# The last expert's outputs kept on the chip: moving gates, loads and return products in a two-block transformer kernel

## The chip, the cores and the metric

The kernel runs on one core of a Trainium2 chip. The metric is the device time of one execution in microseconds (us), taken as the median of three runs. TensorE (PE) multiplies matrices, VectorE (DVE) and ScalarE (ACT) work on elements, GpSimd (POOL) issues indirect transfers, and SyncE (SP) issues the loads and stores in the order in which they stand in its queue.

## The reference: what is computed

The program is two blocks with float32 inputs, model width 1024 and 256 tokens. The second block also carries 256 context tokens. It runs an even mixer (neighbourhood attention and an mLSTM), a first mixture of experts (MoE) over all 512 rows, an odd mixer (attention with grouped queries), and a second MoE over the 256 latent rows. Each MoE has 16 experts, of which a row uses two:

```python
w = jnp.take_along_axis(scores, e_idx, axis=-1)
w = w / w.sum(axis=-1, keepdims=True)
comb = (jax.nn.one_hot(e_idx, N_EXPERTS) * w[..., None]).sum(axis=1)
y = jnp.zeros_like(h)
for e in range(N_EXPERTS):
    y = y + comb[:, e:e + 1] * ((jax.nn.silu(h @ w1[e]) * (h @ w3[e])) @ w2[e])
...
x_lat = x_lat + g2 * y_lat          # in the first MoE: x_ctx = x_ctx + cg2 * y_ctx too
```

So each expert's output row is multiplied with a routing weight and with a gate vector (`g2` for latent, `cg2` for context rows) before it is added to the row's residual `x`.

## The kernel before

The first MoE (`moe_gather`, line 1765) gives each expert 96 slots. For each expert it gathers the rows' inputs from `hbuf` in device memory (`X`, an indirect DMA that GpSimd issues), transposes them (`xtp`, `XT`), multiplies them with four 1 MB slices of `w1` and `w3` into `ph` (slots 0 to 63) and `pq` (slots 64 to 95), applies the SwiGLU gate (`ga`, `gq`), transposes again (`gT`), and multiplies with two 1 MB slices of `w2` into `py` and `pyq`. ScalarE copies these into `ysb` (128x512) and `ysq` (128x256), and SP stores both into `ybuf` in device memory (lines 1834 and 1841). The weights lie in a ring of 18 slots of 1 MB (`SLOTS0`), filled by `wload` (line 343) on the SP queue, in which the two stores of every expert stand too.

The outputs come back per row: `fetch` (line 1852) gathers each row's first expert (`G`, four tiles of 128 rows) after expert 14's store, and its second expert (`qT`, `kT`, `v`) after expert 15's store. `combine` weights a tile with `wn` and the gate (`g2`, line 1860; one tile on ScalarE and GpSimd, lines 1863 and 1864) and adds it to `x` or `xc` (line 1865). Then the odd mixer starts: sum of squares per row on ScalarE (line 390), a power on GpSimd (lines 392 and 394), a diagonal matrix `diag` of the row scales (line 314), transposes of the scaled rows (`htp`), and the projection products `pt`. Its weights are split into a high part `wh` (ScalarE, line 368) and a low part `wl` (VectorE, line 369) in `stream`; the first of them are loaded in six pieces.

The second MoE (`moe_onehot`, line 1880) works without gathers: one-hot matrices bring rows to slots (`px`) and back. `second` makes an expert's weighted output `Y` as a high and a low part, and `back` (line 1975) adds a pair of experts to `x` by products `yc` of K=64 rows: expert rows 0 to 63 of the array hold one half of the columns, rows 64 to 127 the other. `back` is called after the odd expert's `Y`, in the middle of the next expert.

The order on each engine is set by a scheduler that goes by priority and readiness; `issue_after` ties an instruction behind another.

## Time and profile before

| what | us |
|---|---|
| median of three runs | 1564.82 (1559.56 to 1565.23) |
| the profiled execution | 1561.84 |
| its span, first to last instruction | 1560.1 |
| PE busy | 1419.2 (91% of the span) |
| DVE busy | 718.0 (46%) |
| ACT busy | 438.7 (28%) |
| POOL busy | 154.2 (10%) |

The even mixer lies at about 490 to 760 us, the first MoE at 765 to 1117, the odd mixer with its start at 1117 to 1290, and the second MoE from 1290 to the end. A row of a timeline gives start, duration, engine and line, the operation with its output and inputs, the shapes and the count, and in brackets the idle time before it and what ended that. Matrix products are pipelined, so the distance between two starts says more than a duration.

### The profile page before, as it was taken

The numbers are of one execution on the slowest core, as the hardware profiler recorded it, in microseconds if no ns is written. First come the engines' busy times: TensorE is split into PE (matmuls) and PEld (weight loads), VectorE is DVE, ScalarE is ACT, GpSimd is POOL, SyncE is SP. The second block draws the span as 40 slices with busy tenths as digits, with TensorE's granted clock in tenths as the row PEclk, the third lists the DMA queues.
The fourth block names the chain that finished last, engine by engine and source line by source line (L and its number), as shares of the span: only waits on it lengthen the run. The fifth ranks groups of instructions, "written<-read, shape, count | busy, mean of one in ns | idle before, by whom it ended". The sixth has DMA issues, their size and how long they took to land.

```text
span 1560.1 us, 24539 instructions
## 1 busy us (share of the span) xinstructions
PE 1419.2 (91%) x10110; PEld 927.2 (59%) x10110; DVE 718.0 (46%) x1609; ACT 438.7 (28%) x881; POOL 154.2 (10%) x217
## 2 busy tenths in 40 slices
PE   8999999999999998989489999986549998999997
PEld 7576787768888885959433333332238785434342
DVE  4756544866654657365512111011166755333333
ACT  4334332344543324243211111012124432111110
POOL 2100120002101312000110000000142000000000
PEclk9999999999999999989789999998859998999999
DMA  8677675676723112124599878877543528999890
GB/s 298 233 295 284 229 249 174 235 286 231 233 67 95 53 33 79 55 86 158 218 342 338 323 282 325 325 297 298 197 159 109 223 89 317 419 421 418 332 376 30
DMA packets 65703, 359.23 MB, mean 230 GB/s; under 512 B 13027, under 2 KB 16349, under 8 KB 26793
## 3 DMA queue, kind: packets, MB, share of 16 engines
q1 hardware_dynamic: 57680, 335.04, 57.4%
q0 software_dynamic: 5824, 19.68, 3.9%
q10 hardware_dynamic: 2073, 2.79, 0.5%
q8 instruction: 84, 1.38, 0.3%
q14 instruction: 42, 0.34, 0.1%
HBM read 344.77 MB, written 12.71 MB: 229 GB/s over the span
## 4 chain that ended last, share of the span: by engine, by line
PE 37%; DMA 9%; DVE 2%; ACT 1%; issue 1%; SPq 0%; POOL 0%; ACTq 0%; POOLq 0%; DVEq 0%
PE ph L270 14%; PE py L270 6%; DMA w<-in_w_dram 5%; PE pt L270 4%; PE pq L270 3%; DMA ybuf<-ysq 2%; PE yc L270 2%; PE gtp L293 1%; PE px L270 1%; PE pyq L270 1%; PE poG L270 1%; PE lgG L270 1%; PE xtp L293 1%; DMA w<-in_odd_w_dram 1%; PE htp L270 0%
## 5 line engine op out<-in xcount | busy, mean ns | idle before, releaser
L270 PE MATMUL ph<-w,XT 128*64 128x512 f32 x1024 | 256.6, 616 | 28.0 <-DMA w<-in_w_dram 13.9
L369 DVE TENSOR_TENSOR wl<-w,wh 128x2048 fp32r<-128x2048 f32 (+2 forms) x74 | 152.1, 2058 | 104.6 <-ACT wh L368 103.9
L270 PE MATMUL pt<-wh,hT 128*128 128x256 f32 x640 | 187.0, 293 | 0.6 <-ACT hT L368 0.5
L270 PE MATMUL pt<-wl,hT 128*128 128x256 f32 x640 | 185.2, 290 | 1.7 <-DVE wl L369 1.7
L270 PE MATMUL pt<-wh,hTl 128*128 128x256 f32 x640 | 183.2, 290 | 0.7 <-POOL hTl L369 0.2
L368 ACT CAST wh<-w 128x2048 fp32r<-128x2048 f32 (+2 forms) x74 | 127.1, 1719 | 138.5 <-PE pt L270 48.5
L270 PEld LDWEIGHTS ph<-w,XT 128*64 128x64 f32 x1024 | 70.1, 139 | 152.5 <-issue 128.0
L270 PE MATMUL pf<-hT,wh 128*128 128x256 f32 (+1 forms) x480 | 141.5, 299 | 0.3
L270 PE MATMUL pf<-hT,wl 128*128 128x256 f32 (+1 forms) x480 | 140.5, 294 | 1.0 <-DVE wl L369 0.9
L270 PE MATMUL pf<-hTl,wh 128*128 128x256 f32 (+1 forms) x480 | 141.3, 295 | 0.0
L1753 DVE SCALAR_TENSOR_TENSOR ga<-ga,ph 64x512 f32<-64x512 f32 x32 | 21.7, 679 | 235.6 <-ACT ga L1752 235.6
L270 PEld LDWEIGHTS pt<-wl,hT 128*128 128x128 f32 x640 | 123.9, 194 | 9.1 <-issue 5.9
L270 PEld LDWEIGHTS pt<-wh,hT 128*128 128x128 f32 x640 | 123.9, 194 | 8.9 <-issue 4.8
L270 PEld LDWEIGHTS pt<-wh,hTl 128*128 128x128 f32 x640 | 122.9, 193 | 4.4 <-issue 2.6
L270 PE MATMUL py<-w,gT 128*64 128x512 f32 x512 | 121.6, 596 | 1.3 <-DVE gT L1826 0.8
L270 PEld LDWEIGHTS pf<-hT,wh 128*128 128x128 f32 x480 | 91.5, 192 | 11.1 <-issue 4.7
L270 PEld LDWEIGHTS pf<-hT,wl 128*128 128x128 f32 x480 | 92.0, 192 | 7.6 <-issue 2.9
L270 PEld LDWEIGHTS pf<-hTl,wh 128*128 128x128 f32 x480 | 92.1, 192 | 5.5 <-issue 4.2
L270 PEld LDWEIGHTS py<-w,gT 128*64 128x64 f32 x512 | 37.0, 137 | 68.0 <-issue 65.5
L270 PE MATMUL ada<-w,cT 128*32 128x512 f32 x384 | 73.2, 612 | 0.1
L270 PE MATMUL pq<-w,XT 128*32 128x256 f32 x1024 | 72.1, 384 | 0.0
L270 PE MATMUL pt<-wh,yT 128*128 128x256 f32 x256 | 62.6, 289 | 0.0
(525 smaller groups left out, 2136.9 us busy)
## 6 DMA issues: line engine op xcount, KB each, us to landing
w<-in_w_dram SPq DMA_DIRECT2D x192, 1024.0 KB, 12.9
w<-in_ada_w_dram SPq DMA_DIRECT2D x48, 1024.0 KB, 7.2
w<-in_w_in_dram SPq DMA_DIRECT2D x30, 1024.0 KB, 7.3
w<-in_even_w_dram SPq DMA_DIRECT2D x12, 1024.0 KB, 4.8
w<-in_w_out_dram SPq DMA_DIRECT2D x8, 1024.0 KB
w<-in_even_out_dram SPq DMA_DIRECT2D x4, 1024.0 KB, 4.8
ybuf<-ysb SPq DMA_DIRECT2D x16, 256.0 KB
w<-in_odd_w_dram SPq DMA_DIRECT2D x4, 1024.0 KB, 5.0
```

What stands on the lines that cost most here:

```text
L270: self.last = self.nc.tensor.matmul(out, lhsT, rhs, start=start, stop=stop)
L293: self.nc.tensor.transpose(out, in_, self.cst["ident"][:k, :k])
L368: self.nc.scalar.copy(hi, src)
L369: (self.nc.vector if eng == "v" else self.nc.gpsimd).tensor_tensor(out=lo, in0=src, in1=hi.bitcast(F32), op=ALU.subtract)
L1753: nc.vector.scalar_tensor_tensor(g, g, 1.0, ph[0:n], op0=ALU.add, op1=ALU.mult)
```

## The change

In the first MoE, VectorE now applies routing weight and gate to an expert's slots when it reads `py` and `pyq` (`gated`: two fused products and a sum, with the weights of latent and of context rows, `wt`, computed in `route`). The gates per slot (`gs`) are loaded once by twelve DMAs on GpSimd's queue into the ring's slot `hold[2]`, so the ring has 17 slots. The gathers of `X` are issued three experts ahead in the code. Expert 15 is stored no more: its outputs stay in `ysb` and `ysq`, one-hot matrices `oh`, transposed to `ohT`, bring them to the rows by products `yl`, and `x` adds those from PSUM. All eight gathers `G` are issued after expert 14's store; a row that has no slot among the stored ones gets a row of zeros. The odd mixer's first loads and their splits are tied behind the last expert's weights and gates. In the second MoE, `back` issues the products of the two halves of the array in turn, and its call moves behind the first products of the following expert. In the even mixer, `side_by_side` gets a 1x1 product that waits for the bank of a pair (`banks`).

```diff
-SLOTS0 = lambda ...: ... + wx(rz + rx[5:] + hold[1:3])
+SLOTS0 = lambda ...: ... + wx(rz + rx[5:] + hold[1:2])
+YROW = 5 * P
...
-    def side_by_side(self, *streams, after=None):
-        for group in zip(*streams):
-            for m in reversed(group):
-                with self.tc.issue_after(after) if after else ExitStack():
-                    after = self.mm(*m).ins
+    def side_by_side(self, *streams, banks=(), after=None):
+        one = self.cst["ones"][:, :1]
+        for m in [(b[:1, :1], one, one, True, True) for b in banks] + [m for group in zip(*streams) for m in reversed(group)]:
+            with self.tc.issue_after(after) if after else ExitStack():
+                after = self.mm(*m).ins
...
# stream: the first three units of the odd weights
+                with ExitStack() as c:
+                    for ins in after if n < 3 else ():
+                        c.enter_context(self.tc.issue_after(ins))
...
# even mixer, the pair cmb[0], cmb[1]
-                                    for d in range(2)))
+                                    for d in range(2)), banks=cmb[:1])
...
# moe_gather
+            Xs = [fetch_in(e) for e in range(XBUFS)]
+            gs = self.hold[2].tile([P, 2 * D], F32, tag="wx", name="gs")
...
+                        nc.gpsimd.dma_start(g[m * j:m * j + m, w], self.mod[l][w:w + 1, ...].to_broadcast([m, n]))
...
+            def gated(y, py, i, e):
+                g, wt, n = gates[i], self.wt[i], y.shape[-1]
+                yt = T([P, 512], "yt", 1)[:, :n]
+                nc.vector.scalar_tensor_tensor(y, py, wt[:, 0, e:e + 1], g[:, 0], op0=ALU.mult, op1=ALU.mult)
+                nc.vector.scalar_tensor_tensor(yt, py, wt[:, 1, e:e + 1], g[:, 1], op0=ALU.mult, op1=ALU.mult)
+                return nc.vector.tensor_add(y, y, yt).ins
...
-                self.copy(ysb, py, "s")
+                gated(ysb, py, 0, e)
+                if e < NE - 1:
+                    nc.sync.dma_start(self.ybuf[r0:r0 + 64]..., ysb)
...
                 if e == NE - 2:
-                    self.combine_first(l)
-            with self.tc.issue_after(last.ins):
-                for t in range(NT - 1):
-                    self.combine(0, t, self.first[t // 2][:, t % 2], nc.vector)
+                    G = self.fetch_all(NT, rx)
+            self.behind = [self.loaded, shown, gated_]
+            for t in range(NT):
+                with self.tc.issue_after(gated_):
+                    for c in range(2):
+                        nc.vector.tensor_add(xs[t], xs[t], G[c][t // 2][:, t % 2])
+                pos = [self.psum(("lg", "pj")[t % 2], name="yl") for _ in range(2)]
+                for part, (src, n) in enumerate(((ysb, 512), (ysq, 256), (ysq, 256))):
+                    for j in range(2):
+                        q = slice(64 * j, 64 * j + 64)
+                        self.mm(pos[j][:, ...], ohT[q, t, part * P:(part + 1) * P], src[q], part == 0, part == 2)
+                for j in range(2):
+                    nc.vector.tensor_add(o, o, pos[j])       # o: x's columns j
...
# odd_mixer
-            for t in range(4):
-                got = self.fetch(1, t, G[t])
-            with self.tc.issue_after(got.ins):
-                self.combine(0, 3, self.first[1][:, 1], nc.gpsimd)
...
-                self.combine(1, t, g, nc.vector)
...
# moe_onehot
-            def back(pr, owT, Y):
+            def back(pr, owT, Y, after=None):
                 for t in range(NT):
+                    pos = [self.psum(POT[j], name="yc") for j in range(2)]
+                    r = [slice(64 * j, 64 * j + 64) for j in range(2)]
+                    after = self.side_by_side(*([(pos[j], owT[r[j], t, i], Y[i][n][r[j]], i + n == 0, i + n == 2)
+                                                 for i in range(2) for n in range(2)] for j in range(2)), after=after)
...
                     last = hidden(e, tiles[pr][0], w13, 0, ph)
+                    if e % 2 and pr:
+                        back(pr - 1, tiles[pr - 1][1], Ys[-2:], last.ins)
...
-                        if e % 2 == 0:
-                            back(pr - 1, tiles[pr - 1][1], Ys[-2:])
```

The first place where instructions stand otherwise is the SP queue at the end of the first MoE, between the store of expert 11's `ysq` and that of expert 14's. Before:

```order
L1841 DMA ybuf<-ysq 4x32x256
L343 DMA w<-in_w_dram 128x2048 x2
L357 DMA w<-in_odd_w_dram 128x512 x4
L357 DMA w<-in_odd_w_dram 128x1024 x2
L1834 DMA ybuf<-ysb 2x64x512
L343 DMA w<-in_w_dram 128x2048 x2
L1841 DMA ybuf<-ysq 4x32x256
L357 DMA w<-in_odd_w_dram 128x2048
L1834 DMA ybuf<-ysb 2x64x512
L1841 DMA ybuf<-ysq 4x32x256
L357 DMA w<-in_odd_w_dram 128x2048 x2
```

The same stretch of the SP queue now:

```order
L1888 DMA ybuf<-ysq 4x32x256
L345 DMA w<-in_w_dram 128x2048 x4
L1880 DMA ybuf<-ysb 2x64x512
L1888 DMA ybuf<-ysq 4x32x256
L1880 DMA ybuf<-ysb 2x64x512
L1888 DMA ybuf<-ysq 4x32x256
L363 DMA w<-in_odd_w_dram 128x512 x4
L1880 DMA ybuf<-ysb 2x64x512
L363 DMA w<-in_odd_w_dram 128x1024
L1888 DMA ybuf<-ysq 4x32x256
L363 DMA w<-in_odd_w_dram 128x1024
L363 DMA w<-in_odd_w_dram 128x2048
```

The last two slices of expert 15's `w2` stood behind the six odd pieces and a store; now the last four slices of expert 15 stand together, and odd pieces and the stores of experts 12 to 14 follow them.

The second place is VectorE after the last expert. Before, each gathered tile was weighted and then added:

```order
L1826 COPY gT<-gtp 128x4x64
L1860 SCALAR_TENSOR_TENSOR G_10691<-G_10691,wn,g_10688 128x1024
L1865 TENSOR_TENSOR x<-x,G_10691 128x1024
L1860 SCALAR_TENSOR_TENSOR G_10691<-G_10691,wn,g_10688 128x1024
L1860 SCALAR_TENSOR_TENSOR G_10698<-G_10698,wn,g_10688 128x1024
L1865 TENSOR_TENSOR x<-x,G_10691 128x1024
L1865 TENSOR_TENSOR xc<-xc,G_10698 128x1024
L1860 SCALAR_TENSOR_TENSOR qT<-qT,wn,g_10688 128x1024
```

Now, from the last expert's gating of `pyq` on:

```order
L1838 TENSOR_TENSOR ysq<-ysq,yt 128x256
L1897 TENSOR_TENSOR x<-x,G 128x1024 x2
L1897 TENSOR_TENSOR xc<-xc,G 128x1024
L375 TENSOR_TENSOR wl<-w,wh 128x512 x4
L375 TENSOR_TENSOR wl<-w,wh 128x1024 x2
L1897 TENSOR_TENSOR x<-x,G 128x1024 x2
L1897 TENSOR_TENSOR xc<-xc,G 128x1024 x2
L1906 TENSOR_TENSOR x<-x,yl 128x512 x4
L1897 TENSOR_TENSOR xc<-xc,G 128x1024
L1906 TENSOR_TENSOR xc<-xc,yl 128x512 x4
L314 TENSOR_SCALAR hfull<-htp,modA,modc 128x128 x4
```

The weighting is gone, the six odd splits stand between the third and the fourth addition of a gathered tile, and sixteen additions end before the first feature.

The third place is TensorE within a pair of experts of the second MoE; the number behind `Y` tells the expert and the high or low part apart, and lines left out hold other products. Before:

```order
L270 MATMUL yc<-Y_12799,owT 128x512
L270 MATMUL yc<-Y_12800,owT 128x512
...
L270 MATMUL ph<-w,XT 64x512 x5
L270 MATMUL yc<-Y_12934,owT 128x512 x2
L270 MATMUL yc<-Y_12935,owT 128x512 x2
L270 MATMUL yc<-Y_12934,owT 128x512
L270 MATMUL yc<-Y_12935,owT 128x512
L270 MATMUL ph<-w,XT 64x512 x3
```

Now:

```order
L271 MATMUL ph<-w,XT 64x512 x10
L271 MATMUL yc<-Y_13261,owT 128x512 x2
L271 MATMUL yc<-Y_13262,owT 128x512 x2
L271 MATMUL ph<-w,XT 64x512
...
L271 MATMUL yc<-Y_13396,owT 128x512 x2
L271 MATMUL yc<-Y_13397,owT 128x512 x2
L271 MATMUL yc<-Y_13261,owT 128x512
L271 MATMUL py<-w,gT 64x512 x8
...
L271 MATMUL yc<-Y_13261,owT 128x512
L271 MATMUL yc<-Y_13262,owT 128x512 x2
```

An `x2` is now a product on the array's upper rows beside one on its lower rows with the same `Y`. Sixteen products, which stood in groups of 4, 2, 6 and 4, stand in groups of 4, 5 and 7; one product at the end of the second group has its partner at the head of the third.

## Rows read from the trace of the kernel before

**Rows 1.** stretches: busy us (count) per engine, granted clock, DMA share, GB/s

```profile
490.00:565.00 75.00, 75.00 (x527) 63.52 (x526) 44.93 (x114) 26.77 (x48) 20.22 (x40) 1.00 0.14 44
860.00:900.00 40.00, 40.00 (x348) 16.05 (x350) 7.33 (x14) 5.60 (x13) 1.90 (x2) 1.00 0.88 328
1081.70:1092.81 11.11, 0.00 (x0) 0.00 (x0) 4.96 (x6) 5.94 (x10) 0.00 (x0) 0.68 0.66 240
1116.80:1160.02 43.22, 5.83 (x20) 4.65 (x21) 22.27 (x21) 8.62 (x18) 17.39 (x19) 0.53 0.56 198
1330.00:1460.00 130.00, 127.97 (x743) 53.49 (x741) 49.63 (x102) 19.81 (x38) 0.00 (x0) 1.00 1.00 416
1460.00:1524.00 64.00, 61.82 (x358) 25.23 (x356) 20.96 (x36) 9.22 (x18) 0.00 (x0) 1.00 0.84 329
```

**Rows 2.** chain that ended last, 950 to 1072: start, us, what

```profile
1040.63 1.94 PE ph L270 x8
...
1045.88 15.82 DMA w<-in_w_dram
...
1061.84 3.59 PE ph L270 x8
```

**Rows 3.** the same chain from 1070 to 1162

```profile
1080.46 10.11 DMA w<-in_odd_w_dram
...
1117.20 18.94 DMA ybuf<-ysq
...
1141.72 3.80 DVE qT L1860
```

**Rows 4.** timeline of VectorE: start, us, what, count, idle before and releaser

```profile
1086.80 2.60 DVE L369 TENSOR_TENSOR wl<-w,wh 128x512 fp32r<-128x512 f32 x4 [20.11 <-ACT wh L368]
1090.40 2.50 DVE L369 TENSOR_TENSOR wl<-w,wh 128x1024 fp32r<-128x1024 f32 x2 [0.99 <-ACT wh L368]
1092.81 0.67 DVE L1753 SCALAR_TENSOR_TENSOR ga<-ga,ph 64x512 f32<-64x512 f32 x1
...
1137.21 1.22 DVE L1865 TENSOR_TENSOR xc<-xc,G 128x1024 f32<-128x1024 f32 x1
```

**Rows 5.** timeline of GpSimd, the gathers of the first and second expert

```profile
1124.19 1.02 POOL L1852 DMA_INDIRECT G<-ybuf,sidx  x1 [113.49 <-DMA g<-mod]
...
1137.00 1.16 POOL L1852 DMA_INDIRECT qT<-ybuf,sidx  x1 [7.90 <-DMA ybuf<-ysq]
1138.47 0.99 POOL L1852 DMA_INDIRECT qT<-ybuf,sidx  x1 [0.30 <-issue]
```

**Rows 6.** the gathers of the experts' inputs X, last line of that tile's view

```profile
DMA to landing us min/median/max: 4.7/9.2/14.9
```

**Rows 7.** timeline of ScalarE ahead of the odd mixer

```profile
1146.85 1.06 ACT L390 ACTIVATE qT<-x 128x1024 f32<-128x1024 f32 x1 [9.69 <-DMA v<-ybuf,sidx]
...
1156.00 0.40 ACT L314 ACTIVATE diag<-cpack,nrmr 128x128 f32<-128x128 f32 x1 [1.96 <-POOL nrmr L394]
```

**Rows 8.** timeline of TensorE, the odd mixer's first projection product

```profile
1160.02 0.56 PE L270 MATMUL pt<-wh,hT 128*128 128x256 f32 x1
```

**Rows 9.** timeline of TensorE, one pair of experts in the second MoE

```profile
1350.22 1.20 PE L270 MATMUL yc<-Y,owT 64*128 64x512 f32 x6
1351.35 1.50 PE L270 MATMUL ph<-w,XT 128*64 128x512 f32 x5
...
1356.76 1.19 PE L270 MATMUL yc<-Y,owT 64*128 64x512 f32 x4
1357.88 1.51 PE L270 MATMUL px<-oh,xn 128*128 128x128 bf16 x24
...
1366.71 0.71 PE L270 MATMUL yc<-Y,owT 64*128 64x512 f32 x2
1367.35 1.08 PE L270 MATMUL ph<-w,XT 128*64 128x512 f32 x4
```

**Rows 10.** timeline of TensorE, one cmb product of the even mixer

```profile
511.86 1.12 PE L270 MATMUL cmb<-cm,cpack 32*128 32x512 f32 x2
```

More of the change, by code (lines that the diff above doesn't have):

```diff
@@ L39 @@
 BEHIND = (9,)
-FOLLOW = (15, 16, 17)
+FOLLOW = (15, 16)
 H2S = 1
@@ L344, in wload, with stream @@
         return t
-    def stream(self, units):
+    def stream(self, units, after=()):
         nc = self.nc
@@ L1800, in moe_gather @@
                                              bounds_check=NT * P - 1, oob_is_err=False)
+                return X
+            Xs = [fetch_in(e) for e in range(XBUFS)]
+            gs = self.hold[2].tile([P, 2 * D], F32, tag="wx", name="gs")
+            gates = []
+            for m, o in ((64, 0), (32, D)):
+                n = m * 8
+                g = gs[:, o:o + 2 * n].rearrange("p (w f) -> p w f", w=2)
+                for w in range(2):
+                    for j in range(P // m):
+                        nc.gpsimd.dma_start(g[m * j:m * j + m, w], self.mod[l][w:w + 1, 5 * D + n * j:5 * D + n * (j + 1)].to_broadcast([m, n]))
+                gates.append(g)
+            rel = self.last_slots(sidx, C, NT)
+            def gated(y, py, i, e):
[4 more added lines that the diff above has]
+                return nc.vector.tensor_add(y, y, yt).ins
+            for e, (w13, w2) in enumerate(weights):
+                X = Xs.pop(0)
                 XT = T([P, KD, C], "XT", 2)
@@ new lines, in last_onehot @@
+    def last_onehot(self, rel, NT, p0, p1):
+        nc, iota = self.nc, self.cst["iota128"]
+        oh, ohT = (p.tile([P, NT, 3 * P], F32, tag="wx", name=n) for p, n in ((p0, "oh"), (p1, "ohT")))
+        nc.gpsimd.memset(oh, 0.0)
+        for c0, n, i in ((0, 64, 0), (P, 32, 0), (2 * P, 32, 32)):
+            for j in range(2):
+                o = c0 + 64 * j + i
+                s0 = 0 if n == 64 else 64
+                nc.vector.tensor_tensor(oh[:, :, o:o + n], iota[:, None, s0:s0 + n].to_broadcast([P, NT, n]),
+                                        rel.unsqueeze(2).to_broadcast([P, NT, n]), op=ALU.is_equal)
+        for t in range(NT):
+            tp = self.psum("tp", name="ohtp")
+            for i in range(3):
+                self.tr(tp[:, i * P:(i + 1) * P], oh[:, t, i * P:(i + 1) * P])
+            self.copy(ohT[:, t], tp[:, :3 * P], "s")
+        return ohT
@@ new lines, in fetch_all @@
+    def fetch_all(self, NT, rx):
+        G = [[rx[2 * c + w].tile([P, 2, D], F32, tag="wx", name="G") for w in range(2)] for c in range(2)]
+        n = YROW + (NE - 1) * CAP
+        for t in range(NT):
+            for c in range(2):
+                self.nc.gpsimd.indirect_dma_start(out=G[c][t // 2][:, t % 2], out_offset=None, in_=self.ybuf[:n],
+                                                  in_offset=bass.IndirectOffsetOnAxis(ap=self.sidx[:, c, t:t + 1], axis=0),
+                                                  bounds_check=n - 1, oob_is_err=False)
+        return G
@@ L2004, in moe_onehot @@
                     last = hidden(e, tiles[pr][0], w13, 0, ph)
+                    if e % 2 and pr:
+                        back(pr - 1, tiles[pr - 1][1], Ys[-2:], last.ins)
                     if e:
```

116 lines of the change are left out of this document (63 added, 53 removed).

## The prediction, made before the changed kernel was run

> **What bounds the kernel now.** I read the stretches first, then the chain of waits, then the timelines where the chain leaves TensorE.
>
> In the first MoE TensorE is full at first (40.00 of 40 us at 860 to 900 [rows 1]). Later it waits for weights: the chain goes through loads that take 15.8 us from issue to landing, and the experts follow each other at the pace of the transfers, from 1040.63 to 1061.84, 21.2 us [rows 2]. Where only weights move, the rate is 416 GB/s [rows 1], so 1 MB (1.049 million bytes) takes 2.52 us and an expert's six loads 15.1. The other 6.1 us of a period are what the two stores of its outputs cost the queue. They move 0.38 MB, but hold back what is behind them far longer than their bytes.
>
> At the end of this MoE come two stretches with TensorE nearly empty. From 1081.70 to 1092.81 it does nothing [rows 1]: the six odd pieces, the last of which lands at 1080.46 + 10.11 = 1090.57 [rows 3], occupy ScalarE and VectorE (2.60 and 2.50 us of splits [rows 4]) ahead of the last experts' gates. From 1116.80 to 1160.02 it works 5.83 us of 43.22, at a clock of 0.53 [rows 1]: expert 15's store takes 18.94 us [rows 3], gathers, weighting and adding follow, and the first projection starts at 1160.02 [rows 8].
>
> In the second MoE TensorE is full (127.97 of 130 us, then 61.82 of 64), while the transfers run at 1.00 until 1460 and at 0.84 after it [rows 1]. None of its waits there is for a load.
>
> **The change part by part.**
>
> *Gating in slots.* ScalarE's copies go. VectorE gets three operations for each half: 3 x 0.67 us for 512 columns by the nearest form [rows 4], less for 256. VectorE is busy 7.33 us of 40 at 860 to 900 [rows 1], so this hides beside TensorE. The stores are ready about 1.5 us later; with 15.8 us between issue and landing of the loads [rows 2] the transfers do not run dry. I take zero. The twelve loads of `gs` are about 0.79 MB, 1.9 us at 416 GB/s; small rows make it 2.5 by my estimate (0 if they fill gaps, 5 at twice my value). These add to a transfer stream that sets the end.
>
> *One slot fewer, gathers three ahead.* Three buffers of `X` were used before too, so the gathers gain nothing. A slot fewer costs at most one load of 2.52 us where the ring is full at the start; later the loads are late, not the slots. I take 0 (0 to +2.5).
>
> *Odd loads behind the last weights.* The last `w2` slice of expert 15 now lands at 1090.57 - 5.0 (2 MB of odd pieces) + 5.0 (the two `w2` slices that stood behind them) + 2.5 (gates) = 1093.1. TensorE is no longer blocked by splits at 1081.70 to 1092.81; what is late next is these slices, and I put the end of expert 15 near 1107 instead of 1116.80 (the 24.0 us from 1092.81 on, less some 10 for first products and expert 14's outputs that are done by then). This alone does not set the odd mixer's start.
>
> *The return.* The store of 18.94 us, its gathers, and the weighting (3.80 us for the first tile, which ran beside GpSimd's product [rows 3]) leave the chain. What is late next is expert 14's store. Behind 1093.1 stand three pairs of stores (3 x 6.1 = 18.3) and 1.5 MB of odd pieces (3.8): it lands at 1115.2. Before, the first gather started at 1124.19 after the same store [rows 5]. Now eight gathers start at 1116.0, 1.3 us apart (0.99 and an idle 0.30 [rows 5]), and land 9.2 us after issue, as those of `X` do among loads [rows 6]: the fifth at 1130.4, the eighth at 1134.3.
>
> VectorE's order makes the rest: the addition of the fifth gather ends at 1131.7, then the six splits 5.1 us [rows 4] to 1136.8, four additions of 1.2 [rows 4] to 1141.6, four `yl` additions of 512 columns at 0.67 to 1144.3, one of 1.2 to 1145.5, four of 0.67 to 1148.2. ScalarE takes the sums of squares of all four tiles before the first `diag`, so both `diag` of `x` come after 1.3 us more (1.06 [rows 7], and a little to read the sum out), at 1149.5. From the second `diag` to the first `pt` it was 1156.00 to 1160.02, 4.0 us [rows 7, 8]; I add 1.0 because the first tile's transposes now stand there too: 1154.5 instead of 1160.02, **-5.5 us**. From below: a store pair at 4.9 instead of 6.1 and gathers landing in 7 us, between the least and the median of [rows 6], give -10.8. From above: gathers 5 us slower among the loads of odd pieces and of the second MoE give 0.
>
> A rule speaks against this step. First the row: the gather issued at 1137.00, beside an addition of two tensors that ran on VectorE from 1137.21, took 1.16 us, and the next 0.99 [rows 4, 5]; sharing cost 0.17 us. The Trainium skill ("SBUF — State Buffer", section "Who interferes with whom") says that a VectorE instruction with two SBUF inputs and a GpSimd instruction that reads SBUF exclude each other for a whole instruction. By that rule each of the last four gathers could wait for a split or an addition, some 1.2 us, and `pt` would start 5 us later, which is no gain here; by the row it is under 1 us. I go by the row, which is the nearer case.
>
> *Odd mixer.* Its third unit and the first two loads of the second MoE come later than before but are queued by about 1125, before 1154.5; no cost.
>
> *Return products of the second MoE.* Products that stand next to each other on different rows of the array start together: six products from 1350.22 to 1351.35 take 1.13 us, and four, on the same rows in turn, from 1356.76 to 1357.88 take 1.12 [rows 9]; among the six are two such pairs, so both groups have four steps. Two single products take 0.64, from 1366.71 to 1367.35 [rows 9]. So a step costs 0.24 us and a group's edges 0.16. The sixteen products of a pair of experts take 1.13 + 1.12 + 1.12 (a second group of four) + 0.64 = 4.0 us. In groups of 4, 5 and 7 with two, three and four steps they take 0.64 + 0.88 + 1.12 = 2.64. Eight pairs of experts give 8 x 1.36 = 10.9; the last one stands in the tail, where its two halves wait for `Y` anyway, so I take **-10.5 us** (-15 if all sixteen pair up and waits on `Y` go too, -2 if the second half's bank keeps the pairs apart). TensorE sets the time in this stretch. The transfers must not take over: an expert's loads need 15.1 us at 416 GB/s and TensorE some 15.5 an expert now, 14.9 then. The difference of 0.2 us an expert is drawn from a lead that the ring had built up by 1460, where the share falls to 0.84 [rows 1].
>
> *Even mixer.* Three of four `cmb` pairs ran as two products apart from each other, 1.1 us each [rows 10]; joined, three go: -3.3 on an engine that is full (75.00 of 75 [rows 1]). The scheduler reorders the surroundings; I take **-2.5** (-3.3 to +3).
>
> Sum: -5.5 - 10.5 - 2.5 = -18.5 on the profiled 1561.84 (span 1560.1 and 1.7 around it), 1543.3. That execution lies below the median 1564.82 but above the lowest run, so I say 1545.
>
> **The rivals.**
>
> *A: the pairs save nothing.* If the second product of a pair waits for its bank, or the loads become the bound after all, only the start of the odd mixer and the even mixer remain: 1561.84 - 5.5 - 1 = 1555.3. For it: transfers at 1.00 until 1460 [rows 1]. Against it: no wait for loads in that stretch, and pairs seen to start together.
>
> *B: the odd mixer starts much earlier.* If the 6.1 us of a pair of stores are not paid when three pairs, ready since long, are queued together, expert 14's store lands near 1099 and the gathers end by 1115. Then VectorE bounds: from about 1107 its 21 us of additions and splits end near 1130, and `pt` starts near 1137, 23 us earlier: 1561.84 - 23 - 10.5 - 2.5 = 1526. Against it: the period of 21.2 us [rows 2] charges each pair fully.
>
> *C: the gated stores hold the SP queue (slower).* The stores wait for VectorE now, and loads stand behind them in the same queue. If each pair delays the loads by the added 1.5 + 0.9 us, fifteen experts cost 36 us and the sum is +17.5: 1579. It decides where the loads issued before the store have landed by then. Against it: 15.8 us of transfers are in flight [rows 2].
>
> **How the numbers follow.** Forecast 0.57 (1536 to 1553), A 0.18, B 0.17, C 0.08. A change under 0.5% (7.8 us) cannot be told from none here, so "faster" means below 1557.0. Faster: 0.55 of the forecast's 0.57, 0.07 of A, 0.16 of B, 0.78. Slower: most of C, 0.07. Same: the rest, 0.15. The range reaches from 1528, near B, to 1561, past A; it leaves out C and a little at each end.
>
> **What would show it.** Right: no idle TensorE stretch ahead of expert 15's products behind odd splits; eight gathers from about 1116, `pt` near 1155; `yc` groups of three per pair of experts, 2.7 us in sum, and a second MoE shorter by about 10 us. Wrong: TensorE waits for loads in the second MoE (A), gathers before 1105 (B), gaps between loads from 960 to 1060 with a period above 22 us (C).

## The result and the profile after

The changed kernel takes 1578.64 us (median, 1572.88 to 1581.19), the kernel before beside it 1562.19 (1556.92 to 1565.23). The ratio is 1.0108, 95% interval 1.0075 to 1.014: slower by 16.5 us, where 1545 and a gain were predicted. The profiled execution takes 1581.19, its span 1579.4.

Each profile below is one execution, and stages vary between executions: the way to the first store of `hbuf` took 756.0 to 764.0 us in the thirteen traces whose even mixer is that of the kernel before. A few us between two traces therefore say little where that stage is part of the difference.

The stages, from the first starts in the two traces (us):

| stage | before | after |
|---|---|---|
| to the first store of `hbuf` | 763.0 | 767.1 |
| to the first gather of `X` | 16.0 | 19.5 |
| to the first `pyq` (expert 0) | 34.5 | 39.7 |
| 13 experts, `pyq` to `pyq` | 258.6 | 265.4 |
| to the end of expert 15 | 44.5 | 43.3 |
| to the first `pt` of the odd mixer | 43.3 | 47.3 |
| to the first `px` of the second MoE | 145.3 | 147.5 |
| to the end | 254.8 | 249.5 |

The second MoE got 5.3 us shorter and the stretch from expert 13's `pyq` to the end of expert 15 1.2; all other stages got longer. By expert 13's `pyq` 19.5 us are lost (1072.2 before, 1091.7 after).

At the start, TensorE's timeline (start, us, operation, count, idle before and releaser) shows 96 new products for the slots' weights ahead of the branch that all engines pass, and then 14 us without work:

```profile
779.54 2.88 PE L271 MATMUL wslot<-r_t,r_ohf 128*64 128x16 f32 x96 [1.16 <-DVE r_t L1626]
796.66 1.51 PE L295 MATMUL xtp<-cpack,X 96*128 96x96 f32 x8 [14.23 <-DMA X<-hbuf,tab]
```

GpSimd's timeline of the same stretch has two more gathers and the first loads of `gs` behind the first gather:

```profile
786.57 1.13 POOL L1815 DMA_INDIRECT X<-hbuf,tab  x1 [17.09 <-PEq L1801]
788.00 0.96 POOL L1815 DMA_INDIRECT X<-hbuf,tab  x1 [0.30 <-issue]
789.27 0.96 POOL L1815 DMA_INDIRECT X<-hbuf,tab  x1 [0.31 <-issue]
790.23 2.67 POOL L1829 DMA_DIRECT2D gs<-mod  x5
```

The chain that ended last goes through this gather: the first expert's rows are 9.96 us under way, against 4.7 for the fastest gather before [rows 6].

```profile
786.57 9.96 DMA X<-hbuf,tab
796.52 0.14 issue
796.66 1.51 PE xtp L295 x8
```

TensorE's waits from 780 to 1120 (what, for whom, us in total, times, longest) show weights late ten times:

```profile
PE ph L271 <- DMA w<-in_w_dram: 21.5, 10, 3.8
PE xtp L295 <- DMA X<-hbuf,tab: 14.2, 1, 14.2
```

Before, from 772 to 1100, it was five times:

```profile
PE ph L270 <- DMA w<-in_w_dram: 13.9, 5, 6.0
PE xtp L293 <- DMA X<-hbuf,tab: 9.6, 1, 9.6
```

At the end of the first MoE the chain reads as follows. It answers to [rows 3]:

```profile
1088.26 14.41 DMA ybuf<-ysq
...
1124.68 11.42 DMA ybuf<-ysq
...
1142.25 9.05 DMA G<-ybuf,lsidx
...
1162.42 9.08 PE yl L271 x16
...
1182.70 0.85 PE pt L271 x4
```

Expert 14's store lands at 1136.1 (1115.2 was predicted), the eight gathers are 1.3 us apart and the one on the chain lands after 9.05 (9.2 was predicted). Then comes what was not predicted: 18 of the 48 `yl` products run on TensorE only after VectorE's first additions of a `yl`. TensorE's timeline, and under it ScalarE's, which takes the first sum of squares only when the last `yl` is there:

```profile
1162.42 2.07 PE L271 MATMUL yl<-ysb,ohT 64*128 64x512 f32 x2 [21.55 <-DVE x L1906]
```

```profile
1171.58 1.06 ACT L396 ACTIVATE qT<-x 128x1024 f32<-128x1024 f32 x1 [33.14 <-PE yl L271]
```

In the second MoE the three groups of `yc` stand as predicted. The costliest groups from 1330 to the end (busy us, mean ns of one, idle before) and a wait that is new:

```profile
L271 PE MATMUL px<-oh,xn 128*128 128x128 bf16 x384 | 26.2, 224 | 7.1 <-DVE x L2062 5.0 <-DVE wn L1508 2.0
...
L271 PE MATMUL yc<-Y,owT 64*128 64x512 f32 x128 | 25.8, 453 | 2.4 <-DVE x L2062 1.1 <-ACT Y L2048 1.1 <-DVE Y L2049 0.2
```

Before, the same groups were:

```profile
L270 PE MATMUL yc<-Y,owT 64*128 64x512 f32 x128 | 34.4, 432 | 3.2 <-ACT Y L1971 1.9 <-DVE x L1984 1.3
...
L270 PE MATMUL px<-oh,xn 128*128 128x128 bf16 x384 | 24.2, 219 | 1.6 <-DVE wn L1508 1.5
```

`yc` fell by 8.6 us of TensorE's time, and the waits ahead of `px` rose by 5.5, of which 5.0 are for VectorE's additions to `x` (line 2062): by the code `px` and `yc` take the same two PSUM tags, so a `px` now finds its bank still read by the addition of a `yc`.

### The profile page after: what moved, and what is told of

It reads as the page before. It is cut to its first block, busy times and chain, and to the rows that moved or that the text cites. A ratio compares the mean times of both kernels' runs of the same rounds, so it can differ in the third digit from the quotient of the medians.

```text
span 1579.4 us, 24996 instructions
## 1 busy us (share of the span) xinstructions
PE 1438.4 (91%) x10274; PEld 940.2 (60%) x10274; DVE 765.7 (48%) x1720; ACT 427.3 (27%) x854; POOL 154.8 (10%) x230
## 4 chain that ended last, share of the span: by engine, by line
PE 35%; DMA 9%; DVE 3%; issue 1%; SPq 1%; ACT 1%; DVEq 0%; POOLq 0%; ACTq 0%
PE ph L271 13%; DMA w<-in_w_dram 6%; PE py L271 6%; PE pt L271 4%; PE pq L271 3%; DMA ybuf<-ysq 2%; PE yc L271 1%; PE gtp L295 1%; PE px L271 1%; PE pyq L271 1%; PE lgG L271 1%; PE poG L271 1%; DMA G<-ybuf,lsidx 1%; DVE wl L375 1%; DMA X<-hbuf,tab 1%
## 5 line engine op out<-in xcount | busy, mean ns | idle before, releaser
L1770 ACT ACTIVATE ga<-ph 64x512 f32<-64x512 f32 x32 | 18.9, 592 | 261.2 <-PE ph L271 261.2
L1836 DVE SCALAR_TENSOR_TENSOR ysb<-py,wt,gs 128x512 f32<-128x512 f32 x16 | 12.0, 751 | 135.1 <-DMA ybuf<-ysb 93.8
```

The source lines that it names most:

```text
L1770: nc.scalar.activation(g, ph[0:n], AF.Tanh, scale=0.5)
L1836: nc.vector.scalar_tensor_tensor(y, py, wt[:, 0, e:e + 1], g[:, 0], op0=ALU.mult, op1=ALU.mult)
```

## The experiments

### Two parts alone, on the kernel before

Only the odd mixer's first three units tied behind expert 15's store (`b_odd`):

```diff
+                    for ins in after if n < 3 else ():
+                        c.enter_context(self.tc.issue_after(ins))
+            self.behind = [stq, shown]      # the last ysq store, the last gT copy
```

> The kernel before with the odd mixer's first three weight units tied behind the store of expert 15's ysq and nothing else; outputs are returned by stores and gathers. Theory (the store queue sets the return): the last weight lands near 1090.5 instead of 1100.5, four pairs of stores of 6.1 us and the gates g2 end near 1117, the gathers of the second experts start near 1118 instead of 1137.0, the first pt near 1141, total -18, near 1544. Rival (the odd weights are then late and TensorE waits for them): total 1555 or more.

Measured: 1548.61 us, ratio 0.9929 (0.9906 to 0.9952). The second expert's gathers start at 1116.2 instead of 1137.0 [rows 5], and `pt` at 1142.7 instead of 1160.0. But 7.3 us of both lie ahead of the edit: in this execution the first gather of `X` starts at 771.7 instead of 779.0. Counted from there, `pt` starts 10.0 us earlier (371.0 instead of 381.0), and 4.1 of these are lost again in the odd mixer, which takes 149.4 us from `pt` to `px` instead of 145.3. The order of the odd loads moves the odd mixer's start by itself; for the whole kernel it gives 11 us by the ratio (7 to 15), of which this trace shows 6.

Only `back` and its place in the second MoE (`b_back`; the lines of the change):

> The kernel before with the return products of the second MoE as in the changed kernel and nothing else. By the trace of the changed kernel yc takes 22.8 us of TensorE instead of 32.0, and px waits 5.0 us for VectorE's additions: total -5 us, near 1557. By the prediction's step, without the new wait: -10.5, near 1552.

Measured: 1552.21, ratio 0.9946 (0.9922 to 0.997), 8 us by the ratio. The second MoE takes 248.6 instead of 254.8, and the new wait is there as well:

```profile
PE px L270 <- DVE x L1985: 5.0, 5, 1.1
```

Both together (`b_oddback`):

> The kernel before with two parts of the change alone: the odd mixer's first three load units tied behind expert 15's ysq store, and the return products of the second MoE in pairs at the new place. If the two parts act on different stretches, as their single runs show (1548.6 against 1562.2 by the order of the odd loads, which moves the last expert weight from 1100.5 to about 1088, and 1552.2 by the products, which takes the second MoE from 254.8 to 248.6 us), their gains add up: 1548.6 - 8.8 = about 1540, with the first pt near 1142 and the second MoE near 249. Rival: the loads that the first part delays come in the way of the odd mixer and of the second MoE's first weights, and the stretch from the first pt to the second MoE takes 149 to 150 instead of 145; the gains then overlap and the time stays near 1548.

Measured: 1546.13, ratio 0.9889 (0.986 to 0.9919). The stretch from `pt` to `px` takes 148.7 us, as the rival had it; but `b_odd` alone has 149.4, so this is part of what the odd loads cost and no overlap of the two gains. By the ratios the gains add up within the intervals: 0.71% and 0.54% alone, 1.11% together.

### One slot fewer, on the kernel before

```diff
-wx(rz + rx[5:] + hold[1:3])
+wx(rz + rx[5:] + hold[1:2])
```

> The kernel before with one slot fewer (17) in the first MoE's ring and nothing else. Theory (late start: what the changed kernel adds ahead of the first MoE's first product delays the release of the slots, and the ring passes it to the loads): the first product of expert 0 stays at 785.4, the first pyq at 813.6 within 1 us, the total within 4 us of before. Rival (the missing slot starves the loads by itself): loads 7 to 12 land 8 us later, as in the changed kernel, and the total rises by 8 us or more.

Measured: 1582.08, ratio 1.0154 (1.0112 to 1.0196). The 13 experts take 262.0 (+3.4; the five kernels with 18 slots and whole stores in SP's queue range from 255.7 to 260.1 in this stretch). Most of the rest comes from the end: with 17 slots one of expert 15's loads is issued behind the last stores and odd loads, and TensorE waits for it once:

```profile
PE py L270 <- DMA w<-in_w_dram: 27.2, 1, 27.2
```

The changed kernel does not have that order, so the total says little about it; some 3 us in the 13 experts are what remains.

### The start of the first MoE, in the changed kernel

The slots' weights computed behind the branch, after the first gathers (`a_late`):

```diff
-            ohf = T([P, 2 * NT, C], "r_ohf")     # in route, ahead of the branch
+            rel = self.last_slots(sidx, C, NT)
+            self.slots(T)                        # the 96 wslot products, behind the gathers
```

> The changed kernel with the products of the slots' weights (wslot, 96 of them) behind the branch and the first gathers instead of ahead of them (gq has one buffer instead of two to make room). Theory (late start): the first gather starts 3.5 us earlier, near 783, the first pyq 3.5 to 9 us earlier than 826.3, and the total falls by 3.5 to 9 us from 1578.6. Rival (missing slot): the end of the first MoE does not move, and the total stays within 3 us.

Measured: 1573.21, ratio 1.0094 (1.0063 to 1.0125). The way to the first gather falls from 19.5 to 15.6, the products now run while the gather is under way, and the rows are as late as before (9.7 us after the gather's issue):

```profile
780.22 2.88 PE L271 MATMUL wslot<-vwk,XT 128*64 128x16 f32 x96 [6.92 <-DVE lsidx L1931]
787.44 1.51 PE L295 MATMUL xtp<-cpack,X 96*128 96x96 f32 x8 [4.34 <-DMA X<-hbuf,tab]
```

The same with the other two gathers and the `gs` loads held until the first rows have landed (`a_x1`):

```diff
+            seen = nc.gpsimd.tensor_scalar(seen, Xs[0][:, :4], 1.0, 1.0, ...).ins
+            with self.tc.issue_after(seen):
+                Xs += [fetch_in(e) for e in range(1, XBUFS)]      # and the gs loads
```

> The changed kernel with the slots' weights behind the branch, and with the second and third gather of inputs and the gate loads issued only once the first gather has landed (gq has one buffer). Theory (the first gather shares its way with the other gathers and gate loads): it lands 4.4 to 5 us after issue instead of 9.7, the first pyq follows the first gather by 34.6 us as before instead of 39.7, total 5 us under the version with late slot weights alone, near 1568. Rival (the weight loads issued beside it slow it): it still lands after 9 us or more, the first pyq after 39 us or more, total near 1573.

Measured: 1567.24, ratio 1.0048 (1.0018 to 1.0077). From the first gather to the first `pyq` it is 34.3 us, as before the change. GpSimd waits for the rows and then issues the rest; the rows are there 4.8 us after the issue:

```profile
778.47 1.13 POOL L1821 DMA_INDIRECT X<-hbuf,tab  x1 [13.35 <-PEq L1807]
783.25 0.19 POOL L1828 TENSOR_SCALAR seen<-X 96x4 f32<-96x4 f32 x1 [3.64 <-DMA X<-hbuf,tab]
```

This fits the theory, but a later kernel speaks against it. `f_copy` (below) holds the other gathers and the `gs` loads in the same way, and its first rows come as late as in the changed kernel. GpSimd's timeline of `f_copy`:

```profile
774.52 1.13 POOL L1821 DMA_INDIRECT X<-hbuf,tab  x1 [13.27 <-SPq L1807]
784.49 0.19 POOL L1828 TENSOR_SCALAR seen<-X 96x4 f32<-96x4 f32 x1 [8.84 <-DMA X<-hbuf,tab]
```

What goes with the delay in all traces is when SP issues the first weight loads of this stretch. In `f_copy` that is 0.34 us after the gather, in `a_x1` 1.06 (SP's timeline, first `f_copy`, then `a_x1`):

```profile
774.86 25.04 SPq L345 DMA_DIRECT2D w<-in_w_dram  x7
```

```profile
779.53 10.07 SPq L345 DMA_DIRECT2D w<-in_w_dram  x4
```

In the twelve traces in which the first load is issued 1.05 us or more after the gather, the rows land 4.4 to 5.3 us after its issue; in the six in which it is issued between 0.27 us before and 0.68 us after the gather, they land after 9.7 to 10.0. The queues' packets, MB and share in the first 3.5 us after the gather, in `f_copy` (weights, and no rows) and in `a_x1` (q0 the rows, q1 the weights):

```profile
q1 hardware_dynamic: 74, 0.61, 59.4%
```

```profile
q0 software_dynamic: 92, 0.35, 44.0%
q1 hardware_dynamic: 6, 0.05, 4.0%
```

So the rival of this expectation, the weight loads issued beside the gather, agrees with every trace, and the crowding by GpSimd does not. No run moved the loads alone, and why they come 0.4 us later after the gather in `a_x1` than in `a_late` is not shown.

### The `yl` products

Each tile's pair of `yl` in banks that no earlier `yl` holds (`a_yl`):

```diff
-                pos = [self.psum(("lg", "pj")[t % 2], name="yl") for _ in range(2)]
+                pos = [self.psum(u, name="yl") for u in (("lg", "lg"), ("pj", "pj"), ("tp", "tp"), ("pj", "po"))[t]]
```

> The changed kernel with the return products yl of the two context tiles in PSUM banks of their own, so that none waits for VectorE. Theory (the products of the last two tiles, 9.1 us at the low clock behind VectorE's additions, and the sums of squares behind them end the return): all yl end before 1142, the sums of squares follow VectorE's last addition, the first pt comes 6 to 7 us earlier than 1182.35, total near 1572. Rival (the gathers and VectorE's sixteen additions set it): the last gathered tile is added at 1165, pt comes at most 3 us earlier.

Measured: 1570.17, ratio 1.0058 (1.0033 to 1.0083). From the end of expert 15 to `pt` it is 42.7 us instead of 47.3, up to the first `px` of the second MoE 188.2 instead of 194.8, and no `yl` stands behind an addition any more. The trace shows 6.6 us; the medians differ by 8.5, the ratios by 7.8.

### The even mixer

The 1x1 product for the bank taken out (`a_nobanks`):

```diff
-                                    for d in range(2)), banks=cmb[:1])
+                                    for d in range(2)))
```

> The changed kernel without the 1x1 products ahead of the cmb pairs, so the even mixer is as before. Theory by the two traces: the joined pairs save 2.8 us of TensorE, but the mLSTM's first steps come later and lgN, lgC and ntp wait 3.6 us and run longer, so leaving them out takes 2.5 to 3.5 us off: total near 1575.5. The prediction's step says the opposite: +2.5, near 1581.

Measured: 1571.89, ratio 1.0086 (1.0057 to 1.0114). By the medians that is 6.7 us less, by the ratios 3.4, and the intervals overlap. TensorE's row from 490 to 600, and from 592 to 607, in the changed kernel and without the product (first the one, then the other; the granted clock stands third from the end):

```profile
490.00:600.00 110.00, 106.38 (x759) 91.80 (x758) 66.67 (x173) 38.23 (x67) 30.02 (x54) 0.97 0.17 58
592.00:607.00 15.00, 12.95 (x45) 7.43 (x45) 12.02 (x33) 7.35 (x21) 4.27 (x8) 0.54 0.21 72
```

```profile
490.00:600.00 110.00, 108.42 (x768) 91.31 (x768) 66.22 (x172) 37.49 (x67) 27.97 (x48) 1.00 0.15 49
592.00:607.00 15.00, 11.65 (x72) 7.01 (x72) 13.62 (x36) 10.52 (x24) 5.94 (x9) 1.00 0.21 70
```

The joined `cmb` pairs did save time on TensorE (5.07 us with the 1x1 products instead of 7.84), but products elsewhere moved, and TensorE now waits 2.6 us and 1.0 us for ScalarE's `ne` (a step of the mLSTM) where without the product it waits for neither. In all five traces with the product the granted clock stands at 1.2 GHz for 13.7 us right behind the wait of 2.6 us; in the thirteen without it, for 3.4 us at most in that place. On the mean of these traces the way to the first store of `hbuf` is 763.2 us with the product and 760.3 without: some 3 us, in a stage that varies by 8.

### Does gating wait for the stores' buffers?

In the changed kernel VectorE waits long for an earlier store before it may write `ysb` again. Three buffers instead of two (`a_ysb3`):

```diff
-                ysb = T([P, 512], "ysb", 2)
+                ysb = T([P, 512], "ysb", 3)      # ysq too; ga, gq 1
```

> The changed kernel with three buffers instead of two of ysb and ysq (ga and gq one instead of two to make room). Theory (gating on VectorE waits for the store before last, 109.8 us in sum, and holds the next expert's gates in VectorE's queue): the waits go, the time from the first pyq to that of expert 13 falls from 265.4 to about 262, as with 17 slots and no gating, and the last two experts come 3 to 4 us sooner; total -3 to -7, 1572 to 1575. Rival (the stores' and loads' own pace sets it): both stretches stay within 1 us.

Measured: 1578.24, ratio 1.0114 (1.0079 to 1.0149). VectorE's waits from 820 to 1090 in the changed kernel, and with three buffers:

```profile
DVE ysb L1836 <- DMA ybuf<-ysb: 74.7, 7, 13.4
DVE ysb L1836 <- PE py L271: 34.6, 6, 6.7
```

```profile
DVE ysb L1836 <- PE py L271: 78.6, 14, 6.7
```

The wait for the stores is gone and the time is the same: it lay on an engine with time to spare. That theory fell, with one reserve: `ga` and `gq` lose a buffer in the same run, and what that costs was not measured by itself.

### All four costs out, then the gating

The edits of `a_x1`, `a_yl` and `a_nobanks` in one kernel (`a_fix`):

> The kernel after without the four costs found so far: the slot products of the routing moved behind the first gather (-5.4 in its own run), the second and third gather and the gate loads held until the first expert's rows have landed (another -6.0), the yl sums in banks of their own so that VectorE's additions do not hold TensorE (-8.5), and the even mixer's products without the second bank (-6.7). Theory: the four costs lie on the path one behind the other, so 1578.6 - 26.6 = about 1552, with the first expert's pyq 34 us behind the first gather, the first pt some 42 us behind expert 15's end and the stretch of 13 experts still at 264 to 267, since the seventeenth slot is kept. Rival: the gates applied in slots and the return by one-hot products cost more than the stores and gathers that they replace even without these four; then the time stays at 1562 or above.

Measured: 1559.24, ratio 0.9986 (0.9957 to 1.0015). The four give 19 us together, and the time lies between the two theories. The 26.6 is a sum of differences of medians; by the ratios the four give 2.2, 7.2, 7.8 and 3.4 us one by one, 20.6 in all, and by the stages of the traces 3.9, 5.4, 6.6 and some 3, 19 in all. So they do add up; single differences of a few us are within the intervals of about 5 us either way.

The same, with ScalarE's plain copies for experts 0 to 14, which leaves out their weighting and gating (`f_copy`):

```diff
-                gated(ysb, py, 0, e)
+                gated(ysb, py, 0, e) if e == NE - 1 else self.copy(ysb, py, "s")      # ysq too
```

> The combined kernel (a_fix, 1559.2) with the gating in slots left out for experts 0 to 14: ScalarE copies py and pyq into ysb and ysq as before, so the stored outputs are neither weighted nor gated. The gate loads, the seventeen slots, the early gathers and the return by one-hot products stay. Open is the stretch of 13 experts from the first pyq, 267.6 us there against 256.9 in the kernel with the two gains alone. Theory: the stores now wait for VectorE, which adds its three operations and its queue, and hold the loads behind them in the SP queue; then the copies bring the stretch back by 5 or more, to 259 to 262, and the time to 1550 to 1554. Rival: the lost slot and the loads of the gates make the stretch longer, not the gating; then it stays at 265 to 268 and the time at 1557 to 1561.

Measured: 1547.38, ratio 0.9895 (0.9863 to 0.9928). Without gating 12 to 14 us are gone, by the medians and by the ratios, and the 13 experts take 259.2 us instead of 267.6. Experts follow each other at 18.4 us while weights lie ready; `a_fix` first falls behind after expert 7 (25.4 us to the next `pyq`), `f_copy` after expert 8, and from there to expert 14 the mean is 23.1 us in the one and 22.5 in the other.

The traces show only a part of the 12 to 14 us in the experts. In `f_copy` the first `pyq` comes 5.7 us later after the first gather (its rows were late, see `a_x1`), which gives the loads a lead; from the first gather to the end of expert 15 the two executions take the same, 339.4 and 339.9. Over all kernels with whole stores in SP's queue the 13 experts take 263.0 to 267.7 us in the seven with gating and 17 slots, 259.2 and 262.0 in the two with 17 slots and no gating, and 255.7 to 260.1 in the five with 18 slots. By the means the gating is worth some 6 us there and the slot some 3. Where the rest of the 12 to 14 lies is not shown.

Without gating for all experts, without the `gs` loads, and with 18 slots (`f_18`):

> The same without gating for all experts, the gate loads left out and the ring's eighteenth slot back. Theory (the stores behind VectorE): no more than the slot's own 3 us beyond the copies, so the stretch 257 to 259 and the time 1547 to 1551. Rival (slot and gate loads): the stretch falls here alone, from 265 or more to 258, the time to 1549 to 1551. If it stays at 265 here too, it is neither, and the early gathers or the order of the stores are left.

Measured: 1575.04, ratio 1.0075 (1.0045 to 1.0106). The stretch of 13 experts is 255.7, a little less than the 257 to 259 of the theory, but this order again puts last loads behind expert 14's stores (70.5 us from `pyq` 14 to 15). The total is of no use.

### How the gating costs that

The stores on ScalarE's DMA queue, so that no load stands behind them, with gating (`f_actq`) and without (`b_actq`):

```diff
-                nc.sync.dma_start(self.ybuf[...], ysb)
+                nc.scalar.dma_start(self.ybuf[...], ysb)      # ysq too
```

> a_fix (1559.2) with the stores of ysb and ysq issued on ScalarE's DMA queue instead of SP's. Theory (the gated stores hold the loads that stand behind them in SP's queue): the loads no longer wait for a store, the period between experts, where loads set it, falls from 23.3 towards 18.4 to 20, and the time falls by 15 or more, to below 1545. Rival (VectorE itself, or the bytes of the stores, whichever queue they are in): the period stays at 22 to 23.5 and the time at 1552 to 1562.

> b_oddback (1546.1) with the stores on ScalarE's queue, no gating. If the queue is what makes gating dear, this gains less than f_actq does, and the two end within 5 us of each other, apart only by the lost slot: about 1540. If VectorE itself is what costs, both move alike and the difference of 13 us stays.

Measured: 1603.63, ratio 1.0263 (1.0239 to 1.0288), and 1602.39, ratio 1.0267 (1.0229 to 1.0304). Both theories missed. ScalarE now stands still where a store is held up, and the gates behind it are late; from `b_actq`, 820 to 1075:

```profile
ACT ga L1756 <- DMA ybuf<-ysq: 59.1, 5, 11.9
...
PE ph L270 <- ACT XT L302: 53.2, 5, 12.4
```

That the two agree to 1.2 us fits the queue as the place of the gating's cost, but with ScalarE as the bound it proves nothing.

The stores cut into pieces in the same queue, on `b_oddback` (`b_split`):

```diff
-                nc.sync.dma_start(self.ybuf[r0:r0 + 64].rearrange("p (j f) -> j p f", j=2), ysb)
+                for j in range(2):
+                    nc.sync.dma_start(self.ybuf[r0:r0 + 64, 512 * j:512 * (j + 1)], ysb[64 * j:64 * (j + 1)])
# ysq: four pieces of 32 rows in the same way
```

> b_oddback with each store of ysb issued as two and each of ysq as four, one per block of 64 or 32 rows, in the same queue. If the pieces of 64 and 32 rows spread over more DMA engines than the one store does, a pair of stores costs the loads some 2 us instead of 6.1, the period where loads set it falls from 22.7 to about 19, and the time to 1515 to 1530. If a store costs by its place in the queue, six places instead of two make the period longer, 24 or more, and the time 1555 or above.

Measured: 1516.49, ratio 0.97 (0.9669 to 0.973), with the same bytes. Share of the 16 DMA engines (in tenths) and GB/s in 40 slices from 980 to 1050, with the whole stores:

```profile
DMA  9999999941169999999997315999999999214899
GB/s 374 375 421 426 431 407 346 295 145 47 56 150 345 356 342 393 423 435 421 417 424 176 126 52 108 335 362 384 398 437 421 416 431 384 84 61 103 253 394 412
```

and cut:

```profile
DMA  9999999999999999999999999999400339997000
GB/s 391 341 401 435 393 294 324 370 421 403 417 413 439 421 409 412 263 311 384 421 417 417 414 428 435 390 430 412 206 9 0 78 77 177 379 426 295 0 0 0
```

With whole stores the transfers fall, once an expert, to a tenth of the engines and 47 to 61 GB/s at the lowest, for 3.5 to 5 us. SP's timeline of the same kernel shows which store that is: the first dip, near 995 to 999, lies between the issue of `ysb`'s store and that of `ysq`'s, and the two loads between them need 13.51 us to be issued.

```profile
985.01 1.92 SPq L1838 DMA_DIRECT2D ybuf<-ysb  x1
987.48 13.51 SPq L343 DMA_DIRECT2D w<-in_w_dram  x2
1001.08 0.58 SPq L1845 DMA_DIRECT2D ybuf<-ysq  x1
```

Cut, the stores leave no such dip (the two gaps near the end lie where SP has no load to issue, between 1021.9 and 1035.5 and after 1037.4). The median load lands 8.9 us after issue instead of 19.6, and TensorE is busy all 70 us of the window (58.14 before the cut). The first 13 periods are 18.4 us each, the pace of the experts while weights lie ready: TensorE alone sets them. The Trainium skill ("DMA: Bandwidth & Descriptors", section "Why a DMA increments its semaphore by 16 and not by 1") says that a transfer uses as many engines, up to 16, as divide the slowest dimension of both its sides: two for 2x64x512, four for 4x32x256, sixteen for 64 or 32 rows. The share of 0.1 in the dips agrees with two of sixteen; engine by engine it was not looked at.

The same cut in `a_fix` (`f_split`):

> a_fix (1559.2) with the stores cut into the same pieces as in b_split (1516.5). Theory (gating and the lost slot cost only where loads set the pace): the experts follow each other at 18.4 us, the stretch of 13 experts takes 239 as in b_split, and the time falls to 1514 to 1522. Rival (VectorE itself): the stretch stays 8 or more above 239, and the time at 1525 or above.

Measured: 1516.06, ratio 0.9725 (0.9696 to 0.9755), as fast as `b_split`; both are far below the two kernels of this study, and the one-hot return is worth as much there as the stores and gathers it replaces. The windows from 980 to 1050, of `a_fix` cut and of the other cut:

```profile
980.00:1050.00 70.00, 70.00 (x616) 27.99 (x610) 25.69 (x48) 6.85 (x16) 1.91 (x2) 1.00 0.89 336
```

```profile
980.00:1050.00 70.00, 70.00 (x600) 27.64 (x592) 12.75 (x24) 10.11 (x23) 1.92 (x2) 1.00 0.83 316
```

VectorE is busy 25.69 us instead of 12.75 in that window, and TensorE loses nothing by it: the 13 experts take 238.9 in the one and 239.0 in the other. So what gating and slot cost in the experts was a cost to the loads, and goes with their bound.

The kernels in steps, by their ratios to the kernel before:

| kernel | ratio | what the step holds |
|---|---|---|
| `b_oddback` | 0.9889 | odd loads, return products of the second MoE |
| `f_copy` | 0.9895 | + 17 slots, `gs` loads, one-hot return of the last expert |
| `a_fix` | 0.9986 | + gating in slots |
| after | 1.0108 | + slot weights early, first gather beside weight loads, `yl` banks, `cmb` |

## Why the prediction was wrong

**The step that failed** first is "Gating in slots", with its ground that "the transfers do not run dry. I take zero", and with it "I take 0" for slots and gathers. The runs put numbers there. Gating costs some 6 us in the 13 experts by the traces and 12 to 14 in all by the times (`f_copy`, `a_fix`), the lost slot some 3 (`b17`). Two costs were not in the prediction at all: the slot weights ahead of the branch, 3.9 us (`a_late`), and the first gather's rows, 5.4 us late behind weight loads that are issued beside them (`a_x1` and `f_copy`). The error behind the zeros: the prediction itself read that the experts follow each other "at the pace of the transfers", and then costed three edits by TensorE's and VectorE's spare time. Where loads set the pace, whatever delays them is paid expert after expert; at the start, with an empty TensorE, it is paid at once.

The period of 21.2 us that it read is one of several: the five from expert 8's `pyq` to expert 13's range from 18.9 to 26.6, 22.3 on the mean. So the sign that it gave for rival C, "a period above 22 us", was there before the change. That the two stores of an expert "hold back what is behind them far longer than their bytes" was read rightly (`b_split`).

**Even mixer**: -2.5 predicted, about +3 measured on the mean of the traces (+3.4 by the ratios of `a_nobanks`, +4.1 in the two traces of before and after). The pairs joined as foreseen; the moved neighbours, with the waits for `ne` and the clock behind them, cost more.

**The return**: `pt` was predicted at 1154.5 and came at 1182.35. The last weight landed at 1112.6 instead of 1093.1, 19.5 us late, by what had been lost up to expert 13. From there to expert 14's store it was 23.5 us (22.1 predicted), and the gathers landed as foreseen. From the first gather to `pt` it was 45.3 us instead of the 38.5 of the prediction (1116.0 to 1154.5): the sum lacked the products. It let all `yl` stand in PSUM when VectorE came to them, while 18 of the 48 wait for a bank that an earlier sum still holds. With banks of their own the same stretch takes 37.5 us (`a_yl`), so the rest of this sum was right. The rule that the prediction set against this step was hardly tried: all eight gathers had been issued before VectorE's first addition at 1146.21.

**Odd loads**: "This alone does not set the odd mixer's start" was wrong. Alone it moves that start by 10.0 us and gives 11 for the whole kernel by the ratio (`b_odd`).

**Return products of the second MoE**: right in mechanism, too large: -10.5 predicted, -5.3 in the changed kernel and -6.2 alone. TensorE saved 8.6, and the bank shared by `yc` and `px` took back 5.5; transfers did not take over. (The other differences in that stage were not taken apart.)

**The sum of the stages**, after against before: even mixer +4.1, way to the first gather +3.5, from there to the first `pyq` +5.2, the 13 experts +6.8, the rest of the first MoE -1.2, way to `pt` +4.0, odd mixer +2.2, second MoE -5.3. That is +19.3, the difference of the two spans. What the way to `pt` and the odd mixer lost together, 6.2, the edit of `a_yl` gets back (6.6).

**Rival C** gave 1579 and the measured time is 1578.6, but this is chance for the most part. Its mechanism, gated stores that hold the loads, has the right place, at 6 to 14 us of its 36; the rest of the loss lies elsewhere.

**What stays open**: where the part of the gating's 12 to 14 us lies that the experts do not show, and which link makes a gated store dearer to the loads, its later readiness or its place one load earlier in SP's order (one load between `ysb` and `ysq` in `a_fix`, two in `f_copy`). The wait for a store's buffer is excluded (`a_ysb3`), VectorE's busy time as such too (`f_split`); the run that should have told the rest (`f_actq`) made ScalarE the bound. That the weight loads delay the first gather rests on eighteen traces that agree, not on a run that moves the loads alone.

## What to carry to other kernels

Find out for each stage what sets its pace before costing an edit there, and cost it in that currency: 13 us of VectorE's work in 70 cost nothing where TensorE set the pace, and the same gating cost some 6 in the experts, and 12 to 14 in all, where loads did. When a transfer holds the queue longer than its bytes explain, look at its shape first: cutting two stores into pieces by rows gave 29.6 us (1546.13 to 1516.49), more than the two gains of this change together, and the cost of gating and slot in the experts went with it. A product that waits for a bank is as late as the engine that reads the bank. Before calling a cause shown by one pair of traces, look for it in all the others: the hold of `a_x1` seemed to explain the late rows until `f_copy` had the hold and the late rows too.

## What the runs showed of the hardware that was not expected

- A store of 256 KB as 2x64x512 leaves the 16 DMA engines at a tenth of their time and 47 to 61 GB/s for 3.5 to 5 us (`b_oddback`); the same bytes in two pieces of 64 rows leave no such dip (`b_split`).
- An indirect gather of 96 rows lands 4.4 to 5.3 us after issue when the first 1 MB load of the stage is issued 1.05 us or more behind it (twelve traces), and 9.7 to 10.0 us after when that load is issued between 0.27 us before and 0.68 us after it (six traces), one of them with nothing else from GpSimd behind it (`f_copy`).
- After a wait of 2.6 us in the even mixer TensorE's granted clock stands at 1.2 GHz for 13.7 us, in each of five traces.
- A store held up on ScalarE's DMA queue holds ScalarE's arithmetic: 59.1 us of waits in 255, and experts 30 us apart in every second period.
